# The MLP's down projection as seven products of halves, woven between the up projection's tiles

## The chip, the core and the metric

The kernel runs on one core of a Trainium2 chip. The metric is the device time of one execution in microseconds (us). The core has five engines that run side by side and wait for each other through semaphores: TensorE (PE in the profile, its weight loads PEld) multiplies matrices and writes to the eight banks of PSUM; VectorE (DVE), ScalarE (ACT) and GpSimd (POOL) work element by element; SyncE (SP) issues most transfers (DMAs) from HBM into SBUF. Each engine executes its own queue strictly in order.

## The reference

One encoder layer is applied to two groups of 256 tokens with shared weights: three attention branches with gates, an output projection, and then the part that matters here, an MLP with a squared ReLU between two RMS norms. All is float32.

```
    x = x + merged @ w_out
    h2 = rms_norm(x, norm2_g)
    x = x + jnp.square(jax.nn.relu(h2 @ w_up)) @ w_down
    ...
    return rms_norm(x, final_norm_g)
```

D_MODEL is 1024, D_FF is 4096; both groups together are 512 tokens. `w_up` is 1024 x 4096 and `w_down` 4096 x 1024.

## The kernel before

**Precision.** Every large product is made of three matmuls on operands that are split into a high and a low half (`mm3`, line 182): high times high, high times low, low times high. The high half is the operand rounded by a ScalarE copy to TensorE's fast type; the low half is the rest, formed by a subtraction on VectorE. Activations are split in the same way when they are made.

**The order of work.** The program is a list of units. `unit(fn, *srcs)` appends a function and the weight chunks that it needs, and `run` (line 168) executes the list: it sees to it that a unit's chunks are fetched, calls it, and then fetches the chunks of the next units, `ahead` of them (three during the MLP, four at its end). To fetch a chunk (`chunk`, line 160) is to load 128 x 1024 values into one of two `raw` buffers by SyncE, to copy them to `hi` on ScalarE and to subtract into `lo` on VectorE (`halves`). `hi` and `lo` come from ten `w` buffers.

VectorE, ScalarE and TensorE are wrapped in `InOrder` (line 62): what they execute is in the order in which the program writes it. GpSimd (`G`) and SyncE (`SP`) are not wrapped; a planner decides when their instructions come in their queues, and it also hands out the buffers of a pool and puts in every wait. A tile that is taken from a full pool waits for the last reader of the tile whose place it gets.

**The MLP** starts at line 817. The residual `X1` (1024 x 512, features on partitions) and the split activations `H` stand ready.

- `up` (line 837) makes one tile of 128 rows of the hidden layer for all 512 tokens: 24 matmuls (`fm`, 8 x 3), then the ReLU out of the bank on ScalarE, the square on VectorE, and its two halves (`u`).
- `turn_x1` (line 821) transposes the residual on TensorE, after the first eight up tiles, into the sums `acc`, which have tokens on partitions; ScalarE also forms the sums of squares for the norm (`ss`; `inv_ms` makes `rr` from them). The norm's factor is applied at the end: `rr` scales the down projection's result.
- The hidden layer is worked off in four quarters of 1024 (`qq`). After a quarter's eight up tiles come its down products (`tm`, line 194): for each half of the 1024 outputs, four chunks of weights, each with 24 matmuls (four token tiles x two blocks of 128 x three), into four banks. Then `add_down` adds a bank, times `rr`, to `acc` by one VectorE instruction per token tile.
- The last half of the last quarter is `last_down` (line 877): it takes its four chunks first and goes token tile by token tile, with the last tile in two halves of 256 columns. After each token tile `final` normalizes it and sends it out: reduction and scaling on VectorE, the power on GpSimd, then ScalarE and VectorE scale a half each, and two DMAs write it.

`flush` executes what was put into the list `later`: work out of banks that is issued behind the next unit's matmuls.

Of the kernel before, what the change touches and what calls it, by code (L numbers as in the profile page):

```python
# [77 lines left out]
def encoder_kernel(ctx: ExitStack, tc: tile.TileContext, a: dict, out: bass.AP):  # L78
    nc = tc.nc
    V, A, E = (InOrder(tc, e) for e in (nc.vector, nc.scalar, nc.tensor))  # L80
    G, SP = nc.gpsimd, nc.sync

    sb = ctx.enter_context(tc.tile_pool(name="sb", bufs=1))
    ps = ctx.enter_context(tc.tile_pool(name="ps", bufs=8, space=bass.MemoryType.PSUM))
    dr = ctx.enter_context(tc.tile_pool(name="dr", bufs=1, space=bass.MemoryType.DRAM))

    cnt = [0]

    def nm(s):
        cnt[0] += 1  # L90
        return f"{s}{cnt[0]}"

    def s4(s="s"):
        return sb.tile([P, 2, T], F32R, tag="s4", name=nm(s), bufs=21)

    def h2(s="h", dt=F32):
        return sb.tile([P, T], dt, tag="h2", name=nm(s), bufs=20)

    def bank(s="ps"):
        return ps.tile([P, 512], F32, tag="ps", name=nm(s))  # L100

    def const(s, shape, dt=F32):
        return sb.tile(shape, dt, name=s, tag=s, bufs=1)
# [4 lines left out]
    def f(x):  # L108
        return x.bitcast(F32)

    def wide(s):
        return sb.tile([P, 512], F32, tag="bias", name=nm(s), bufs=3, padded_shape=[P, 768])

    PHS = ((0, 4), (4, NPH))
    oh = [wide("oh") for _ in PHS]
# [21 lines left out]
    p = bank("warm")  # L137
# [6 lines left out]
    def unit(fn, *srcs):  # L144
        units.append((fn, srcs))

    def raw_tile():
        return sb.tile([P, 1024], F32, tag="raw", name=nm("raw"), bufs=2)

    def w_tile():  # L150
        return sb.tile([P, 1024], F32R, tag="w", name=nm("w"), bufs=10)
# [8 lines left out]
    def chunk(src, n=1024):  # L160
        raw, hi, lo = raw_tile(), w_tile(), w_tile()
        SP.dma_start(raw[:, :n], src)
        halves(raw, hi, lo, slice(0, n))
        return hi, lo

    ahead = [1]

    def run():
        need = [(i, s) for i, (_, srcs) in enumerate(units) for s in srcs]
        got, at = [[] for _ in units], 0  # L170
        done = 0
        for i, (fn, srcs) in enumerate(units):
            done += len(srcs)
            for fetch in (True, False):
                while at < min(len(need), done + (0 if fetch else ahead[0])):
                    u, s = need[at]
                    got[u].append(chunk(*s))
                    at += 1
                if fetch:
                    fn(*got[i])  # L180

    def mm3(o, wh, wl, xh, xl, first, last):
        E.matmul(o, wh, xh, start=first, stop=False)
        E.matmul(o, wh, xl, start=False, stop=False)
        E.matmul(o, wl, xh, start=False, stop=last)

    def fm(w, X, o):

# [70 lines left out]
    later = []  # L259
# [170 lines left out]


    def sm_tile():
        return sb.tile([P, 2, 384], F32, tag="sp", name=nm("sp"), bufs=3)

    def bias_tile():
        return sb.tile([P, 2, 384], F32, tag="bias", name=nm("bias"), bufs=3)

    biases = []

# [99 lines left out]
            E.matmul(o, QQ[:, e, c], K[:, e, k], start=(n == 0), stop=(n == 1))  # L539

    def turn_two(s):
        t = sb.tile([P, 2, 512], F32R, tag="pT", name=nm("pT"), bufs=2)
        two(turn(s, 0, 2), t[:, 0], t[:, 1])
        return t

# [109 lines left out]
    def flush(n=2):  # L655
        for fn in later[:n]:
            fn()
        del later[:n]
# [45 lines left out]
    def put_v12(t, p):  # L704

        b, i = divmod(t, 2)
        for rl in range(2):
            v = sb.tile([P, S], F32, tag="v12", name=nm("v12"), bufs=8)
            A.activation(v[HALF[0]], p[HALF[rl], :S], AF.Copy)
            V.tensor_copy(v[HALF[1]], p[HALF[rl], S:])  # L710
            V12[b, 2 * i + rl] = v
# [102 lines left out]
        unit(out_proj, (a["w_o"][ff],))  # L814


    acc = {}
    ss = const("ss", [P, NT, 2])
    rr = const("rr", [P, NT])

    def turn_x1(t, hh):

        b = bank("tp")
        for i in range(4):
            E.transpose(b[:, i * P:(i + 1) * P], X1[4 * hh + i][:, t * P:(t + 1) * P], ident)
        acc[t, hh] = h2("acc")
        A.activation(acc[t, hh], b, AF.Copy)
        A.activation(wide("junk"), b, AF.Square, accum_out=ss[:, t, hh:hh + 1])

    def inv_ms():  # L830
        V.tensor_tensor(rr, ss[:, :, 0], ss[:, :, 1], op=ALU.add)
        V.tensor_scalar(rr, rr, 1.0 / D, EPS, op0=ALU.mult, op1=ALU.add)
        V.reciprocal(rr, rr)

    U = {}

    def up(w, qq, ff):
        p = bank()
        fm(w, H, p)
        r = h2("r")  # L840
        A.activation(r, p, AF.Relu)
        V.tensor_tensor(r, r, r, op=ALU.mult)
        u = s4("u")
        A.activation(u[:, 0], r, AF.Copy)
        V.tensor_tensor(u[:, 1], r, f(u[:, 0]), op=ALU.subtract)
        U.setdefault(qq, []).append(u)

    gf = []
    fs = const("fs", [P, NT, 3])
    fr = const("fr", [P, NT])  # L850

    def load_gf():
        for hh in range(2):
            g = wide("gf")
            A.dma_start(g, bass.AP(tensor=a["gf"].tensor, offset=a["gf"].offset + hh * T, ap=[[0, P], [1, T]]))
            gf.append(g)

    def add_down(t, hh, p, last=False):
        y = acc[t, hh]
        V.scalar_tensor_tensor(y, p, rr[:, t:t + 1], y, op0=ALU.mult, op1=ALU.add)  # L860
        if last:
            A.activation(wide("junk"), y, AF.Square, accum_out=fs[:, t, 0:1])
            V.tensor_tensor(y, y, gf[hh], op=ALU.mult)

    def final(t, c, n):
# [4 lines left out]
        G.tensor_tensor(r, r, mhalf[:, 0:1], op=ALU.pow)  # L870
        V.tensor_tensor(acc[t, 1][:, c], acc[t, 1][:, c], gf[1][:, c], op=ALU.mult)
        A.activation(acc[t, 0], acc[t, 0], AF.Copy, scale=r)
        V.tensor_scalar(acc[t, 1], acc[t, 1], r, None, op0=ALU.mult)
        for hh in range(2):
            (A, SP)[hh].dma_start(out[t * P:(t + 1) * P, hh * 512:(hh + 1) * 512], acc[t, hh])

    def last_down(*ws):

        flush(NT)
        Uq = U[3]  # L880
        for t in range(NT):
            c = slice(t * P, (t + 1) * P)
            cols = ((0, 512),) if t < NT - 1 else ((0, 256), (256, 512))
            for part, (n0, n1) in enumerate(cols):
                p = bank()[:, :n1 - n0]
                for k in range(KD):
                    wh, wl = ws[k // 2]
                    w = slice((k % 2) * 512 + n0, (k % 2) * 512 + n1)
                    mm3(p, Uq[k][:, 0, c], Uq[k][:, 1, c], wh[:, w], wl[:, w], k == 0, k == KD - 1)
                y = acc[t, 1][:, n0:n1]  # L890
                V.scalar_tensor_tensor(y, p, rr[:, t:t + 1], y, op0=ALU.mult, op1=ALU.add)
                A.activation(wide("junk")[:, n0:n1], y, AF.Square, accum_out=fs[:, t, 1 + part:2 + part])
                if n1 < 512:
                    V.tensor_tensor(y, y, gf[1][:, n0:n1], op=ALU.mult)
            final(t, slice(n0, n1), 1 + len(cols))

    for qq in range(4):
        for ff in range(KD):
            unit(lambda w, qq=qq, ff=ff: up(w, qq, ff), (a["w_up"][8 * qq + ff],))
            if qq == 0:  # L900
                unit(lambda ff=ff: turn_x1(ff // 2, ff % 2))
        if qq == 0:
            unit(inv_ms)
            unit(load_gf)
        uq = U.setdefault(qq, [])
        if qq == 3:
            unit(lambda: ahead.__setitem__(0, 4))
        for hh in range(2):
            srcs = [a["w_dn"][qq, hh, i] for i in range(4)]
            if qq == 3 and hh:  # L910
                unit(last_down, *[(s,) for s in srcs])
            else:
                def after(t, p, hh=hh, qq=qq):
                    if qq < 3:
                        add_down(t, hh, p)
                    else:
                        later.append(lambda: add_down(t, hh, p, True))

                for u in tm(uq, srcs, 512, after):
                    unit(*u)  # L920
    run()


# [72 lines left out]
```

## Time and profile before

| what | us |
|---|---|
| median of three runs | 872.12 (872.07 to 872.5) |
| the profiled execution's own time | 871.41 |
| its span, first to last instruction | 869.6 |
| first up tile's first matmul | 510.88 |
| last matmul of the MLP ends | 863.30 |

The span is the time from the first to the last instruction; the execution's own time has 1.8 us more around it. In the profile a line of a group names the source line, the engine, the operation, what is written from what (`w<-raw,w` is the low half of a weight, `ps` a bank), the shapes, the count, and then busy time, mean duration in ns, and the idle time of the engine just before with what ended it. Source line 72 is the wrapper of `InOrder`, so operations on the three wrapped engines are told apart by their tiles. Matmuls are pipelined: the recorded duration of one is longer than the pace at which they follow each other, which is read from the chain of work or from the timeline.

### The profile page before, as it was taken

What the parts mean: (1) busy time and instruction counts of PE and PEld (TensorE: products, weight loads), DVE (VectorE), ACT (ScalarE), POOL (GpSimd) and SP (SyncE); (2) the same over time, 40 slices, a digit from 0 to 9 for tenths busy, and PEclk for the clock granted to TensorE, in tenths of its full rate; (3) what the DMA queues carried; (4) which work ended last, traced back from release to release, by engine and by line L of the source; (5) the groups of instructions that cost most, each with busy time, mean ns of one, the idle gap of its engine ahead of it and who ended that gap; (6) DMA issues with size and microseconds to landing.
All of it is one profiled execution on the core that took longest, in us unless ns stands there. A gap on an engine that the chain in (4) does not pass through costs nothing.

```text
span 869.6 us, 10683 instructions
## 1 busy us (share of the span) xinstructions
PE 858.7 (99%) x4176; PEld 717.3 (82%) x4176; DVE 390.1 (45%) x625; ACT 344.7 (40%) x606; POOL 192.6 (22%) x133
## 2 busy tenths in 40 slices
PE   9999999999999999999999999999999999999997
PEld 8778998888888888888887888888888888888886
DVE  6595445456443213333436444433453345334543
ACT  6364555565654332232224335521342144214432
POOL 2315455547556551112212000000000000000001
PEclk9999999999999999999999999999999999999999
DMA  8342223233332122222323432332223222322222
GB/s 284 113 136 88 83 73 103 80 93 98 106 94 71 51 87 96 96 86 97 121 73 99 149 117 96 122 119 74 95 98 121 74 95 98 123 73 93 97 77 98
DMA packets 41851, 88.00 MB, mean 101 GB/s; under 512 B 18734, under 2 KB 18980, under 8 KB 41800
## 3 DMA queue, kind: packets, MB, share of 16 engines
q1 hardware_dynamic: 39272, 83.07, 29.3%
q10 hardware_dynamic: 2304, 4.20, 1.5%
q8 instruction: 33, 0.54, 0.3%
q14 instruction: 18, 0.15, 0.1%
q0 software_dynamic: 224, 0.05, 0.0%
HBM read 85.15 MB, written 2.14 MB: 100 GB/s over the span
## 4 chain that ended last, share of the span: by engine, by line
PE 88%; DVE 4%; ACT 2%; DMA 2%; issue 2%; POOL 1%; SPq 0%; POOLq 0%; DVEq 0%; ACTq 0%
PE ps L72 81%; PE sc L72 3%; PE o L72 2%; PE tp L72 2%; DMA mr<-in_memT 1%; DMA raw<-in_w_mem 1%; ACT sp L72 1%; DVE sp L72 1%; DVE w L72 1%; DVE mg L72 0%; ACT w L72 0%; DVE st L72 0%; DVE qq L72 0%; DVE kl L72 0%; DVE sq L72 0%
## 5 line engine op out<-in xcount | busy, mean ns | idle before, releaser
L72 PE MATMUL ps<-x,w 128*128 128x512 f32 x1080 | 252.4, 391 | 0.0
L72 PEld LDWEIGHTS ps<-x,w 128*128 128x128 f32 x1080 | 200.8, 188 | 41.5
L72 DVE TENSOR_TENSOR w<-raw,w 128x1024 fp32r<-128x1024 f32 (+1 forms) x107 | 131.3, 1234 | 128.7 <-ACT w L72 128.6
L72 ACT ACTIVATE w<-raw 128x1024 fp32r<-128x1024 f32 (+2 forms) x144 | 149.1, 1040 | 95.4 <-DMA raw<-in_w_dn 37.4
L72 PE MATMUL ps<-h,w 128*128 128x512 f32 x768 | 176.7, 390 | 0.0
L72 PE MATMUL ps<-w,u 128*128 128x512 f32 (+1 forms) x792 | 175.1, 383 | 0.0
L72 PEld LDWEIGHTS ps<-w,u 128*128 128x128 f32 x792 | 145.5, 188 | 29.0
L72 PEld LDWEIGHTS ps<-h,w 128*128 128x128 f32 x768 | 143.6, 188 | 29.6
L158 POOL TENSOR_TENSOR w<-raw,w 128x1024 fp32r<-128x1024 f32 (+1 forms) x37 | 87.3, 2361 | 117.8 <-ACT w L72 95.0
L870 POOL TENSOR_TENSOR fr<-fr,mhalf 128x1 f32<-128x1 f32 x4 | 3.5, 870 | 395.9 <-DVE fr L72 395.9
L72 ACT ACTIVATE r<-ps 128x512 f32<-128x512 f32 x32 | 19.1, 598 | 114.4 <-PE ps L72 114.4
L72 DVE TENSOR_TENSOR r<-r 128x512 f32<-128x512 f32 x32 | 22.1, 692 | 70.8 <-ACT r L72 70.8
L72 ACT ACTIVATE sp<-sp,st 128x256 f32<-128x256 f32 (+1 forms) x48 | 25.8, 538 | 57.7 <-DVE st L72 57.7
L72 DVE SCALAR_TENSOR_TENSOR acc<-ps,rr,acc 128x512 f32<-128x512 f32 (+1 forms) x33 | 24.2, 733 | 54.3 <-PE ps L72 54.3
L72 PE MATMUL ps<-mg,w 128*128 128x512 f32 x192 | 44.3, 390 | 1.5 <-ACT mg L72 0.9
L72 ACT ACTIVATE g<-ps 128x512 f32<-128x512 f32 x16 | 9.6, 598 | 91.0 <-PE ps L72 91.0
L72 PEld LDWEIGHTS ps<-mg,w 128*128 128x128 f32 x192 | 36.0, 188 | 9.6 <-ACT mg L72 1.3
L72 PE MATMUL ps<-w,x 128*128 128x384 f32 (+1 forms) x192 | 39.9, 363 | 0.0
L72 DVE TENSOR_TENSOR sum<-o,lo 64x256 f32<-64x256 f32 x24 | 10.0, 418 | 66.5 <-ACT lo L72 66.4
L457 POOL TENSOR_TENSOR sp<-sp,st 128x512 f32<-128x512 f32 (+1 forms) x32 | 36.7, 1147 | 6.5 <-DVE st L72 3.6
L72 PEld LDWEIGHTS ps<-w,x 128*128 128x128 f32 x192 | 34.3, 188 | 3.6
L72 DVE TENSOR_TENSOR u<-r,u 128x512 fp32r<-128x512 f32 x32 | 22.2, 692 | 22.4 <-ACT u L72 22.4
(135 smaller groups left out, 814.4 us busy)
## 6 DMA issues: line engine op xcount, KB each, us to landing
raw<-in_w_up SPq DMA_DIRECT2D x32, 512.0 KB, 3.2
raw<-in_w_dn SPq DMA_DIRECT2D x32, 512.0 KB, 3.3
raw<-in_w_g SPq DMA_DIRECT2D x24, 512.0 KB, 3.3
raw<-in_w_b SPq DMA_DIRECT2D x12, 512.0 KB, 3.2
raw<-in_w_bam SPq DMA_DIRECT2D x8, 512.0 KB, 3.2
raw<-in_w_o SPq DMA_DIRECT2D x8, 512.0 KB, 3.3
raw<-in_w_mem SPq DMA_DIRECT2D x7, 512.0 KB, 4.3
bias<-scr SPq DMA_DIRECT2D x48, 64.0 KB, 3.0
```

The costliest lines, as they stand in the source:

```text
L72: return self.tc.keep_in_program_order(method(*args, **kw))
L158: sub[0].tensor_tensor(lo[:, c], raw[:, c], f(hi[:, c]), op=ALU.subtract)
L457: G.tensor_tensor(s[:, :, :w], s[:, :, :w], st[:, 6:8].unsqueeze(2).to_broadcast([P, 2, w]), op=ALU.mult)
L870: G.tensor_tensor(r, r, mhalf[:, 0:1], op=ALU.pow)
```

## The change

Seven products of halves take the place of eight (Strassen's scheme in a form with shared sums). The hidden layer is now worked off in eight chunks `c` of 512. For each, the 512 tokens, the 512 hidden rows and the 1024 outputs are each cut in two halves, and the product of a 2 x 2 by a 2 x 2 arrangement of blocks is made from seven products of blocks and sums of blocks. A product is 2 (token tiles) x 2 (blocks of 128) x 3 matmuls of 512 columns, twelve in all.

- `up` keeps the square in float32, and makes it on GpSimd. The split into halves is moved to `form`.
- `load_blocks(c)`, called in the third up tile of each chunk, loads the chunk's four weight blocks (128 x 1024 each, the same bytes as before) into eight `blk` buffers and makes four sums of them on GpSimd: a, b, c, d. `parts` splits one of the seven into halves when it is fetched, three units ahead, as other weights are.
- `form(c, n)` makes the left operand of product n: for n = 0 four sums on GpSimd, and for each n the split of one form on ScalarE and VectorE.
- The order of units in loop step c: the four up tiles of chunk c, then the seven products of chunk c - 1, after each of them `form(c, n)`. The last step has the seven products of chunk 7 alone.
- `product` puts P1, Q5, Q6 and P7 into new pairs of banks (a, d, c, e); P2 goes on in P1's pair, Q3 in Q5's and Q4 in P7's. After its matmuls it flushes what the product before left: two sums on VectorE, each adding a bank to one of five accumulators of two tiles (`add_to`; the first use of an accumulator is a copy on ScalarE, which may carry the sign).
- In the last step `last_sums` takes the place of `add_to`: it puts the accumulators together, scales them by `rr` onto the residual and, for the last four products, ends the four token tiles (`finish`, `final`).
- The transposed residual is written to DRAM by `turn_x1` (now after the up tiles of chunks 0 and 1) and fetched again before the last products (`fetch_x1`). Buffers that only attention used are given back, and the `blk` buffers take their place (`mlp_pool`).

The core of the diff:

```
+    def load_blocks(c):
+        t = {n: block_tile() for n in ("11", "12", "a", "22", "b", "c", "21", "d")}
+        for n, (k, h) in (("11", (0, 0)), ("12", (0, 1)), ("22", (1, 1)), ("21", (1, 0))):
+            SP.dma_start(t[n], a["w_dn"][c // 2, h, 2 * (c % 2) + k])
+        G.tensor_tensor(t["a"], t["11"], t["12"], op=ALU.add)
+        G.tensor_tensor(t["b"], t["a"], t["22"], op=ALU.add)
+        G.tensor_tensor(t["c"], t["12"], t["22"], op=ALU.add)
+        G.tensor_tensor(t["d"], t["b"], t["21"], op=ALU.add)
+        blocks[c] = t
...
     def up(...):
...
-        V.tensor_tensor(r, r, r, op=ALU.mult)
-        u = s4("u")
-        A.activation(u[:, 0], r, AF.Copy)
-        V.tensor_tensor(u[:, 1], r, f(u[:, 0]), op=ALU.subtract)
+        G.tensor_tensor(UP[c, m // 2][:, m % 2], r, r, op=ALU.mult)
+        if m == 2:
+            load_blocks(c)
...
+    def parts(c, n):
+        def go():
+            hi, lo = w_tile(), w_tile()
+            src = blocks[c][n]
+            A.activation(hi, src, AF.Copy)
+            V.tensor_tensor(lo, src, f(hi), op=ALU.subtract)
+            return hi, lo
+        return go
...
+    def form(c, n):
+        lo, hi = UP[c, 0], UP[c, 1]
+        A11, A21, A12, A22 = lo[:, :, :S], lo[:, :, S:], hi[:, :, :S], hi[:, :, S:]
+        if n == 0:
+            for m in (1, 2, 4, 5):
+                forms[c, m] = h2("f").rearrange("p (j t) -> p j t", j=2)
+            G.tensor_tensor(forms[c, 1], A21, A22, op=ALU.subtract)
+            G.tensor_tensor(forms[c, 2], A11, forms[c, 1], op=ALU.subtract)
+            G.tensor_tensor(forms[c, 4], A11, A21, op=ALU.subtract)
+            G.tensor_tensor(forms[c, 5], A12, forms[c, 2], op=ALU.subtract)
+        src = {0: A11, 3: A12, 6: A22}[n] if n in (0, 3, 6) else forms[c, n]
+        x = s4("f")
+        xh, xl = (x[:, i].rearrange("p (j t) -> p j t", j=2) for i in range(2))
+        A.activation(xh, src, AF.Copy)
+        V.tensor_tensor(xl, src, f(xh), op=ALU.subtract)
+        forms[c, n] = x
+
+    def add_to(k, i, p, op=ALU.add):
+        if (k, i) in acc:
+            V.tensor_tensor(acc[k, i], acc[k, i], p, op=op)
+        else:
+            acc[k, i] = h2("acc")
+            A.activation(acc[k, i], p, AF.Copy, scale=1.0 if op == ALU.add else -1.0)
+
+    PRODUCTS = (("P1", "11", "a", ("V", -1)), ("Q5", "a", "d", ("G", 1)), ("Q6", "b", "c", ("V", 1)),
+                ("P2", "21", "a", ("11", 1)), ("P7", "c", "e", ("G", -1)), ("Q3", "22", "d", ("12", 1)),
+                ("Q4", "d", "e", ("21", 1)))
+
+    def product(w, c, n):
+        name, _, bk, (to, sign) = PRODUCTS[n]
+        x = forms.pop((c, n))
+        new = name in ("P1", "Q5", "Q6", "P7")
+        for i in range(2):
+            if new:
+                banks[bk, i] = bank()
+            p = banks[bk, i]
+            for j in range(2):
+                t = slice(j * S + i * P, j * S + (i + 1) * P)
+                k = slice(j * 512, (j + 1) * 512)
+                mm3(p, x[:, 0, t], x[:, 1, t], w[0][:, k], w[1][:, k], new and j == 0, j == 1, not new)
+        flush(9)
+        ps_ = [banks[bk, i] for i in range(2)]
+        if c < NC - 1:
+            later.append(lambda: [add_to(to, i, ps_[i], ALU.add if sign > 0 else ALU.subtract) for i in range(2)])
+        else:
+            later.append(lambda: last_sums(name, ps_))
...
+    def last_sums(name, ps_):
+        for i in range(2):
+            p, lo, hi = ps_[i], i, i + 2
+            y = {(t, hh): xt[t][:, hh] for t in (lo, hi) for hh in range(2)}
+            if name == "P1":
+                scaled(y[lo, 0], lo, 0, acc["11", i])
+                add_to("V", i, p, ALU.subtract)
+            elif name == "Q5":
+                add_to("G", i, p)
+            elif name == "Q6":
+                add_to("V", i, p)
+                for k in ("12", "G"):
+                    V.tensor_tensor(acc[k, i], acc[k, i], acc["V", i], op=ALU.add)
+                V.tensor_tensor(acc["21", i], acc["21", i], acc["V", i], op=ALU.subtract)
+                scaled(y[lo, 1], lo, 1, acc["12", i])
+                scaled(y[hi, 1], hi, 1, acc["G", i])
+                scaled(y[hi, 0], hi, 0, acc["21", i])
+            elif name == "P2":
+                finish(lo, 0, y[lo, 0], p)
+            elif name == "P7":
+                finish(hi, 1, y[hi, 1], p, -1)
+            elif name == "Q3":
+                finish(lo, 1, y[lo, 1], p)
+                final(lo)
+            else:
+                finish(hi, 0, y[hi, 0], p)
+                final(hi)
+
+    def finish(t, hh, y, p, sign=1):
+        scaled(y, t, hh, p, sign)
+        A.activation(h2("junk"), y, AF.Square, accum_out=fs[:, t, hh:hh + 1])
+        V.tensor_tensor(y, y, gf[0][:, hh], op=ALU.mult)
...
+    for c in range(NC + 1):
+        if c < NC:
+            for m in range(4):
+                unit(lambda w, ff=4 * c + m: up(w, ff), (a["w_up"][4 * c + m],))
...
+        for n in range(7):
+            unit(lambda w, c=c - 1, n=n: product(w, c, n), (parts(c - 1, PRODUCTS[n][1]),))
+            if c < NC:
+                unit(lambda c=c, n=n: form(c, n))
+    unit(lambda: flush(9))
```

`scaled` is one VectorE instruction: source times `rr` (or minus `rr`), plus the residual tile. `final` adds the two sums of squares, scales (VectorE), takes the power (GpSimd), scales a half each on ScalarE and VectorE, and sends both out.

More of the change, by code (lines that the diff above doesn't have):

```diff
@@ L85, in encoder_kernel @@
     dr = ctx.enter_context(tc.tile_pool(name="dr", bufs=1, space=bass.MemoryType.DRAM))
+    stages = ExitStack()
+    at = [stages.enter_context(tc.tile_pool(name="at", bufs=1))]
+    ctx.callback(stages.close)
     cnt = [0]
@@ L111, in wide @@
     def wide(s):
-        return sb.tile([P, 512], F32, tag="bias", name=nm(s), bufs=3, padded_shape=[P, 768])
+        return at[0].tile([P, 512], F32, tag="bias", name=nm(s), bufs=3, padded_shape=[P, 768])
     PHS = ((0, 4), (4, NPH))
@@ L176, in run @@
                     u, s = need[at]
-                    got[u].append(chunk(*s))
+                    got[u].append(s[0]() if callable(s[0]) else chunk(*s))
                     at += 1
@@ L180, in run, with mm3 @@
                     fn(*got[i])
[L182 to L185, printed above, removed]
+    def mm3(o, wh, wl, xh, xl, first, last, more=False):
+        E.matmul(o, wh, xh, start=first, stop=False, skip_group_check=more)
+        E.matmul(o, wh, xl, start=False, stop=False, skip_group_check=more)
+        E.matmul(o, wl, xh, start=False, stop=last, skip_group_check=more)
     def fm(w, X, o):
@@ L432, in sm_tile @@
     def sm_tile():
-        return sb.tile([P, 2, 384], F32, tag="sp", name=nm("sp"), bufs=3)
+        return at[0].tile([P, 2, 384], F32, tag="sp", name=nm("sp"), bufs=3)
     def bias_tile():
-        return sb.tile([P, 2, 384], F32, tag="bias", name=nm("bias"), bufs=3)
+        return at[0].tile([P, 2, 384], F32, tag="bias", name=nm("bias"), bufs=3)
     biases = []
@@ L541, in turn_two @@
     def turn_two(s):
-        t = sb.tile([P, 2, 512], F32R, tag="pT", name=nm("pT"), bufs=2)
+        t = at[0].tile([P, 2, 512], F32R, tag="pT", name=nm("pT"), bufs=2)
         two(turn(s, 0, 2), t[:, 0], t[:, 1])
@@ L707, in put_v12 @@
         for rl in range(2):
-            v = sb.tile([P, S], F32, tag="v12", name=nm("v12"), bufs=8)
+            v = at[0].tile([P, S], F32, tag="v12", name=nm("v12"), bufs=8)
             A.activation(v[HALF[0]], p[HALF[rl], :S], AF.Copy)
@@ L814, in encoder_kernel, with mlp_pool, block_tile @@
         unit(out_proj, (a["w_o"][ff],))
-    acc = {}
+    NC = 8
     ss = const("ss", [P, NT, 2])
     rr = const("rr", [P, NT])
+    nr = const("nr", [P, NT])
+    fs = const("fs", [P, NT, 2])
+    fr = const("fr", [P, NT])
+    x1d = dr.tile([NT, P, D], F32, name="x1d")
+    def mlp_pool():
+        stages.close()
+        at[0] = stages.enter_context(tc.tile_pool(name="ml", bufs=1))
+    def block_tile():
+        return at[0].tile([P, 1024], F32, tag="blk", name=nm("blk"), bufs=8)
     def turn_x1(t, hh):
@@ L825, in turn_x1 @@
             E.transpose(b[:, i * P:(i + 1) * P], X1[4 * hh + i][:, t * P:(t + 1) * P], ident)
-        acc[t, hh] = h2("acc")
-        A.activation(acc[t, hh], b, AF.Copy)
-        A.activation(wide("junk"), b, AF.Square, accum_out=ss[:, t, hh:hh + 1])
+        x = h2("xt")
+        A.activation(x, b, AF.Copy)
+        A.activation(h2("junk"), b, AF.Square, accum_out=ss[:, t, hh:hh + 1])
+        A.dma_start(x1d[t, :, hh * 512:(hh + 1) * 512], x)
     def inv_ms():
@@ L833, in inv_ms, with up @@
         V.reciprocal(rr, rr)
-    U = {}
-    def up(w, qq, ff):
+        V.tensor_scalar(nr, rr, -1.0, None, op0=ALU.mult)
+    UP, blocks = {}, {}
+    def up(w, ff):
+        c, m = divmod(ff, 4)
+        if m % 2 == 0:
+            UP[c, m // 2] = sb.tile([P, 2, T], F32, tag="s4", name=nm("u"), bufs=21)
         p = bank()
@@ L841, in up @@
         A.activation(r, p, AF.Relu)
-        V.tensor_tensor(r, r, r, op=ALU.mult)
-        u = s4("u")
-        A.activation(u[:, 0], r, AF.Copy)
-        V.tensor_tensor(u[:, 1], r, f(u[:, 0]), op=ALU.subtract)
[L846 to L865, printed above, removed]
+        G.tensor_tensor(UP[c, m // 2][:, m % 2], r, r, op=ALU.mult)
[10 more added lines that the diff above has]
+        blocks[c] = t
@@ new lines, in parts @@
+    def parts(c, n):
[6 more added lines that the diff above has]
+        return go
+    forms = {}
+    def form(c, n):
[14 more added lines that the diff above has]
+        forms[c, n] = x
@@ new lines, in encoder_kernel @@
+    acc, banks = {}, {}
+    def add_to(k, i, p, op=ALU.add):
[7 more added lines that the diff above has]
+                ("Q4", "d", "e", ("21", 1)))
@@ new lines, in encoder_kernel, with fetch_x1, scaled @@
+    xt, gf = {}, []
+    def fetch_x1():
+        for t in range(NT):
+            xt[t] = sb.tile([P, 2, 512], F32, tag="s4", name=nm("xt"), bufs=21)
+            SP.dma_start(xt[t], x1d[t].rearrange("p (h n) -> p h n", h=2))
+        g = sb.tile([P, 2, 512], F32, tag="s4", name=nm("gf"), bufs=21)
+        SP.dma_start(g, bass.AP(tensor=a["gf"].tensor, offset=a["gf"].offset, ap=[[0, P], [T, 2], [1, T]]))
+        gf.append(g)
+    def scaled(y, t, hh, src, sign=1):
+        V.scalar_tensor_tensor(y, src, (rr if sign > 0 else nr)[:, t:t + 1], y, op0=ALU.mult, op1=ALU.add)
@@ L867, in final @@
+    def finish(t, hh, y, p, sign=1):
+        scaled(y, t, hh, p, sign)
+        A.activation(h2("junk"), y, AF.Square, accum_out=fs[:, t, hh:hh + 1])
+        V.tensor_tensor(y, y, gf[0][:, hh], op=ALU.mult)
+    def final(t):
         r = fr[:, t:t + 1]
-        V.tensor_reduce(r, fs[:, t, :n], axis=AX.X, op=ALU.add)
+        V.tensor_tensor(r, fs[:, t, 0:1], fs[:, t, 1:2], op=ALU.add)
         V.tensor_scalar(r, r, 1.0 / D, EPS, op0=ALU.mult, op1=ALU.add)
         G.tensor_tensor(r, r, mhalf[:, 0:1], op=ALU.pow)
-        V.tensor_tensor(acc[t, 1][:, c], acc[t, 1][:, c], gf[1][:, c], op=ALU.mult)
@@ L872, in final @@
-        A.activation(acc[t, 0], acc[t, 0], AF.Copy, scale=r)
-        V.tensor_scalar(acc[t, 1], acc[t, 1], r, None, op0=ALU.mult)
+        A.activation(xt[t][:, 0], xt[t][:, 0], AF.Copy, scale=r)
+        V.tensor_scalar(xt[t][:, 1], xt[t][:, 1], r, None, op0=ALU.mult)
         for hh in range(2):
[L875 to L920, printed above, removed]
+            (A, SP)[hh].dma_start(out[t * P:(t + 1) * P, hh * 512:(hh + 1) * 512], xt[t][:, hh])
@@ new lines, in encoder_kernel @@
+    unit(mlp_pool)
+    for c in range(NC + 1):
+        if c < NC:
+            for m in range(4):
+                unit(lambda w, ff=4 * c + m: up(w, ff), (a["w_up"][4 * c + m],))
+                if c == 0:
+                    unit(lambda m=m: turn_x1(m, 0))
+                if c == 1:
+                    unit(lambda m=m: form(0, m))
+                    unit(lambda m=m: turn_x1(m, 1))
+                if c == 2 and m == 0:
+                    unit(inv_ms)
+        if c == 1:
+            for n in range(4, 7):
+                unit(lambda n=n: form(0, n))
+        if c == 0:
+            unit(lambda: ahead.__setitem__(0, 3))
+            continue
+        if c == NC:
+            unit(fetch_x1)
+        for n in range(7):
+            unit(lambda w, c=c - 1, n=n: product(w, c, n), (parts(c - 1, PRODUCTS[n][1]),))
+            if c < NC:
+                unit(lambda c=c, n=n: form(c, n))
```

## The prediction

> **What bounds the kernel now.** I read the page's totals, then the chain that ended last in order of time, then the groups by shape, then the timeline of the end.
>
> ```profile
> span 869.6 us, 10683 instructions
> ...
> PE 858.7 (99%) x4176; PEld 717.3 (82%) x4176; DVE 390.1 (45%) x625; ACT 344.7 (40%) x606; POOL 192.6 (22%) x133
> 516.92 5.47 PE ps L72 x24
> 522.39 0.44 PE tp L72 x4
> 558.33 299.24 PE ps L72 x1320
> 857.57 0.02 issue
> 510.88 5.61 PE L72 MATMUL ps<-h,w 128*128 128x512 f32 x24
> 862.78 0.52 PE L72 MATMUL ps<-w,u 128*128 128x256 f32 x3
> L72 PE MATMUL ps<-h,w 128*128 128x512 f32 x768 | 176.7, 390 | 0.0
> L72 PE MATMUL ps<-w,u 128*128 128x512 f32 x744 | 169.4, 389 | 0.0
> L72 PE MATMUL ps<-w,u 128*128 128x256 f32 x48 | 5.9, 283 | 0.0
> ```
>
> The MLP runs from 510.88 us (first up tile) to 863.30 (last matmul, 862.78 + 0.52). In it TensorE never stops: one piece of the chain holds 1320 matmuls in 299.24 us, so a 512-wide matmul costs 0.2267 us of path (its recorded 390 ns is pipelined). The last token tile's 48 half-wide ones took 863.30 - 857.57 = 5.73. All else hides, until the last 6.3 us to the end of the span at 869.6.
>
> **What is removed.** The down projection has 744 + 48 matmuls; seven products of 2 x 2 x 3 in each of eight chunks make 672 wide ones. Gone are 72 x 0.2267 = 16.3 and 5.7: **-22.0 us**. The up tiles and the eight transposes stay. That gain is real only if the others keep pace with a product, 12 x 0.2267 = 2.72 us, where a pair of weight halves served 24 matmuls before.
>
> **What is added to VectorE.**
>
> ```profile
> L72 DVE TENSOR_TENSOR w<-raw,w 128x1024 fp32r<-128x1024 f32 x64 | 77.8, 1224 | 44.7 <-ACT w L72 44.7
> L72 DVE TENSOR_TENSOR u<-r,u 128x512 fp32r<-128x512 f32 x32 | 22.2, 692 | 22.4 <-ACT u L72 22.4
> 467.21 1.28 DVE L72 TENSOR_TENSOR g<-ps,g 128x512 f32<-128x512 f32 x2
> L72 ACT ACTIVATE w<-raw 128x1024 fp32r<-128x1024 f32 x64 | 66.9, 1050 | 77.1 <-DMA raw<-in_w_dn 37.4 <-DMA raw<-in_w_up 20.4 <-PE ps L72 19.3
> L72 ACT ACTIVATE u<-r 128x512 fp32r<-128x512 f32 x32 | 20.2, 633 | 24.3 <-DVE r L72 24.3
> L72 ACT ACTIVATE r<-ps 128x512 f32<-128x512 f32 x32 | 19.1, 598 | 114.4 <-PE ps L72 114.4
> ```
>
> Between two products it executes, in written order: **D**, two sums from banks (like g<-ps,g, two in 1.28); **S**, the low half of a weight (1.22), three units ahead; **F**, the low half of the next chunk's form (0.69). Sum 3.19 against 2.72: over seven products 22.3 against 19.0. An up tile needs only one S in 24 x 0.2267 = 5.44, so the lag heals there. ScalarE needs 1.05 + 0.63 per product, less than 2.72. POOL gets four squares, four form sums (1.29 each, from a row below) and four block sums (2.42): 20 us of a chunk's 180 x 0.2267 = 41. Those two are no bound by themselves.
>
> The lag bites at one wait. P7 and Q4 share a bank pair (e), with only Q3 between. Q4 may not write until VectorE has summed P7, and that D is queued behind everything of the products before it. Let 0 be the start of P1; Q4 is due at 6 x 2.72 = 16.3. S of the third product can start at 1.7 (relu 0.60, copy 1.05, behind the last up tile). Up to the first half of P7's D stand 6 S, 5 F, 5 D and 0.69: 1.7 + 7.3 + 3.5 + 6.4 + 0.7 = 19.6. So even undisturbed Q4 waits 3.3 us. What is queued behind Q4 on TensorE is the next up tile.
>
> **POOL gets in the way.**
>
> ```profile
> L72 DVE TENSOR_TENSOR mg<-g,mg x5: 679/1777/1786, 461.5 to 471.5; 128x512 fp32r<-128x512 f32 x5
> L783 POOL TENSOR_TENSOR mg<-g,mg x3: 1295/1749/1750, 461.4 to 464.4; 128x512 fp32r<-128x512 f32 x3
> 461.49 5.80 DVE L72 TENSOR_TENSOR mg<-g,mg 128x512 fp32r<-128x512 f32 x4
> L72 DVE TENSOR_TENSOR g<-ps,g x16: 675/692/692, 337.7 to 467.8; 128x512 f32<-128x512 f32 x16
> L158 POOL TENSOR_TENSOR w<-raw,w 128x1024 fp32r<-128x1024 f32 x33 | 80.0, 2424 | 104.4 <-ACT w L72 84.8 <-DVE mk L72 19.4
> L773 POOL TENSOR_TENSOR g<-g,g 128x512 f32<-128x512 f32 x7 | 9.1, 1293 | 92.0 <-DVE g L72 92.0
> raw<-in_w_dn SPq DMA_DIRECT2D x32, 512.0 KB, 3.3
> ```
>
> At 461.5, where merge splits on both engines at once, VectorE's 0.68 becomes 1.78 and POOL's 1.30 becomes 1.75: each waits out the other's instruction, in turn. Both read two SBUF tiles. S and F are of that kind, and so are POOL's squares and form sums (1.29 each) and block sums (2.42). D has one input in a bank; that form never exceeded 0.69. The Trainium skill, "SBUF — State Buffer", Who interferes with whom, states this as an exclusive lock for a whole instruction, for a VectorE operation with two SBUF inputs and not for one; by it the sum is the 940 below, without it the 896 of a rival.
>
> POOL's four form sums are ready at 2.0, after the square of the last up tile. Its sums b, c, d for the next chunk need block 22, whose buffer is free only after this chunk's S for Q3, plus 3.3 to land: S ends at 14.7, so b could start at 18.0, and finds F ahead of it until 18.6. Walked with alternation (end of each VectorE step, POOL in brackets):
> S 3.2 [form sum 4.5], D(Q4 before) 4.5, S 5.7 [7.0], F 7.7, D(P1) 9.0 [9.0], S 10.2 [11.5], F 12.2, D(Q5) 13.5, S 14.7, F 15.4, D(Q6) 16.7, S 17.9, F 18.6 [b 21.0], D(P2) 19.9, S 22.2 [c 24.6], F 25.3, D(P7) 26.0 and 26.6.
> Q4 runs 26.0 to 28.7 instead of ending at 19.0: **+9.7** in each of six full phases, 58.2. In the first phase ten sums go to ScalarE as first copies, four D fewer (5.1) before P7's: Q4 starts near 20.9, **+4.6**. Bounds per full phase: 3.3 (no contention) and, if POOL's two rounds and the clock (below) come on top, about 12.
>
> **The end.** The last two rows of products stand back to back, with no up tiles to heal the lag.
>
> ```profile
> 857.59 0.75 DVE L72 SCALAR_TENSOR_TENSOR acc<-ps,rr,acc 128x512 f32<-128x512 f32 x1 [2.01 <-PE ps L72]
> 859.13 0.15 DVE L72 TENSOR_REDUCE fr<-fs 128x1 f32<-128x2 f32 x1 [0.79 <-ACT junk L72]
> 859.32 0.15 DVE L72 TENSOR_SCALAR fr<-fr 128x1 f32<-128x1 f32 x1
> 859.56 0.93 POOL L870 TENSOR_TENSOR fr<-fr,mhalf 128x1 f32<-128x1 f32 x1 [4.49 <-DVE fr L72]
> 860.52 0.49 DVE L72 TENSOR_SCALAR acc<-acc,fr 128x512 f32<-128x512 f32 x1 [0.44 <-POOL fr L870]
> 865.52 0.48 DVE L72 TENSOR_SCALAR acc<-acc,fr 128x512 f32<-128x512 f32 x1 [0.44 <-POOL fr L870]
> ```
>
> From scaling a tile (857.59) VectorE waits for ScalarE's square until 859.13 (1.54); the gain multiply, in line there, adds 0.69: 2.23 per tile for P2 and P7. For Q3 and Q4 each half also makes a token tile final: 859.13 to 861.01, 1.88 more, 4.1 together. VectorE's list: Q4's old D 1.28, P1 2 x (0.75 + 0.69) = 2.9, Q5 1.28, Q6 2 x (4 x 0.69 + 3 x 0.75) = 10.0, four S 4.9, P2 and P7 8.9, Q3 and Q4 16.4: 45.7. After the last scaling 869.6 - 866.0 = 3.6 remain (output). VectorE enters 32.8 - 28.7 = 4.1 late (after P7's D: d until 27.7, S 28.9, F 29.6, D 30.9, S 32.1, F 32.8). End at 53.4 from the start of these products; TensorE alone would end at 19.0 + 6.3 = 25.3: **+28.1**. Back-to-back instructions start up to 0.08 early, worth 2 to 3 of this; the end has no other cover.
>
> **Clock.**
>
> ```profile
> 863.40:866.00 2.60, 0.00 (x0) 0.00 (x0) 1.55 (x5) 0.99 (x3) 0.66 (x1) 0.90 0.00 0
> 866.00:869.60 3.60, 0.00 (x0) 0.00 (x0) 0.01 (x1) 0.24 (x1) 0.00 (x0) 0.50 0.38 146
> ```
>
> With TensorE idle from 863.30 the granted clock is halved from about 865.5. A wait of 9.7 would reach that; no row shows matmuls behind such an idle time. Bounds for seven waits: 0 and 7 x 2.72 = 19 (each Q4 at half speed). I take 0, since in every row with matmuls the clock was 1.00, and keep 19 for the range. The Trainium skill, "TensorE: Matmul & The Clock Gate", Part 1, gives about 3.4 us at half rate after such a pause; an estimate by that page is 1.7 per wait, 12 in all, and the sum would be 952.
>
> **Costed at nothing:** the x1 round trip through DRAM and its DMAs (beside up tiles; late fetches have 19 us of products), the same 32 down loads, bank slots (each product's new pair finds four free), the pool change. Without cover the fetch would cost some 3 us once.
>
> **Sum**, against the profiled execution's own 871.4 (span 869.6 and 1.8 around it; the median of the runs is 872.1, 0.7 above): 871.4 - 22.0 + 58.2 + 4.6 + 28.1 = **940**.
>
> **Rivals.**
> - *The block sums fall elsewhere.* If b, c, d run under the up tiles, the walk loses their two waits: D(P7) reaches half at 22.5, Q4 ends at 25.2, 6 x 6.2 + 1.1 = 38; entry to the end 3.0 late, 27. 871.4 - 22 + 38 + 27 = 914. For it: POOL's order is the planner's. Against: block 22 comes free in the middle of the products.
> - *No contention worth counting*: 6 x 3.3 = 20, and 27: 896. Against: the mg rows.
> - *Faster: VectorE's order isn't the written one.* If P7's D is done by 16.3 (that is the deciding point) nothing waits, and if the waits for squares (8 x 0.85) and powers (4 x 0.96) at the end are filled, 45.7 becomes 35, +13 with no lag: 871.4 - 22 + 13 = 862. For it: TensorE has 99% and VectorE 45%. Against: VectorE is issued in written order, and 3.19 per product is over 2.72 in either order.
> - *Worse*: clock and ScalarE's queue waiting for POOL's forms: 952 to 975.
>
> **Chances.** Forecast 0.46, block sums elsewhere 0.22, no contention 0.12, worse 0.12, faster 0.07, within 0.2% 0.01. About 0.2% is what a measurement of this kernel can tell from no change. Slower 0.92. The range 888 to 965 takes in 896, 914, 940 and the clock's 19; it leaves out faster, and the worst.
>
> **What would show it.** Right: TensorE idle once per chunk before Q4, released by VectorE's sum of P7; S and F stretched to 2 us or more beside POOL; after the last matmul VectorE busy for 15 us or more. Wrong: TensorE still at 99%, or the idle time before another product, or released by a weight split or a DMA.

## The result, and the profile after

| | before | after |
|---|---|---|
| median (range), us | 872.25 (872.07 to 872.5, 4 runs) | 963.44 (961.51 to 964.04, 4 runs) |
| ratio | | 1.1041, 95% interval 1.1022 to 1.1061 |
| profiled execution (span), us | 871.41 (869.6) | 961.51 (959.6) |
| TensorE instructions | 4176 | 4056 |

The change makes the kernel 10.4% slower, although it takes away 120 matmuls, as it says (744 + 48 - 672). The page of the changed kernel, its totals and its slices (tenths busy of 40 equal slices; PEclk is the granted clock):

```profile
span 959.6 us, 10832 instructions
...
PE 862.4 (90%) x4056; PEld 712.0 (74%) x4056; DVE 518.6 (54%) x724; ACT 381.3 (40%) x662; POOL 384.2 (40%) x229
...
PE   9999999999999999999999997959597795959582
...
PEclk9999999999999999999999998979899897979795
```

TensorE has holes at even distances from the 25th slice on (576 us); the first product begins at 558.68. In the changed kernel the seven products of a chunk stand in a row, behind four up tiles. The view of the waits sums up what TensorE's matmuls waited for (us in total, times, longest):

```profile
PE ps L72 <- DVE acc L72: 64.3, 7, 9.7
PE ps L72 <- DVE xt L72: 6.6, 1, 6.6
PE ps L72 <- DVE w L72: 5.4, 8, 2.0
```

Seven waits for VectorE's sums out of banks, one in each row of products but the last, which waits for `xt`. The timeline of TensorE and then of VectorE over one chunk in the middle:

```profile
694.17 5.46 PE L72 MATMUL ps<-w,f 128*128 128x512 f32 x12 [9.67 <-DVE acc L72]
699.42 22.38 PE L72 MATMUL ps<-h,w 128*128 128x512 f32 x96
721.64 13.99 PE L72 MATMUL ps<-w,f 128*128 128x512 f32 x61
736.13 2.81 PE L72 MATMUL ps<-w,f 128*128 128x512 f32 x11 [0.50 <-DVE w L72]
748.59 4.35 PE L72 MATMUL ps<-w,f 128*128 128x512 f32 x12 [9.65 <-DVE acc L72]
```

```profile
724.56 1.28 DVE L72 TENSOR_TENSOR acc<-acc,ps 128x512 f32<-128x512 f32 x2
...
728.60 1.27 DVE L72 TENSOR_TENSOR acc<-acc,ps 128x512 f32<-128x512 f32 x2
...
732.65 1.27 DVE L72 TENSOR_TENSOR acc<-acc,ps 128x512 f32<-128x512 f32 x2
733.84 2.23 DVE L72 TENSOR_TENSOR w<-blk,w 128x1024 fp32r<-128x1024 f32 x1
736.00 2.88 DVE L72 TENSOR_TENSOR f<-f,f 128x512 fp32r<-128x512 f32 x1
738.80 1.27 DVE L72 TENSOR_TENSOR acc<-acc,ps 128x512 f32<-128x512 f32 x2
740.00 2.17 DVE L72 TENSOR_TENSOR w<-blk,w 128x1024 fp32r<-128x1024 f32 x1
742.09 2.82 DVE L72 TENSOR_TENSOR f<-u,f 128x512 fp32r<-128x512 f32 x1
744.84 1.27 DVE L72 TENSOR_TENSOR acc<-acc,ps 128x512 f32<-128x512 f32 x2
...
747.77 1.27 DVE L72 TENSOR_TENSOR acc<-acc,ps 128x512 f32<-128x512 f32 x2
```

Read them together. The four up tiles (x96) end at 721.6, where P1 begins. Six products follow; the last twelve matmuls of a chunk, Q4's, start 9.65 us late, at 748.59. VectorE runs through without a pause meanwhile; its sums come in the order Q4 of the chunk before, P1, Q5, Q6, P2, P7. The first of P7's two sums ends at about 748.45 (747.77 and 0.68), and Q4 starts 0.14 behind it. A form's low half that needs 0.68 alone takes 2.88 at 736.00. POOL's timeline shows what stands against it there:

```profile
723.63 2.17 POOL L902 TENSOR_TENSOR f<-u,u 128x512 f32<-128x512 f32 x1
725.88 2.25 POOL L903 TENSOR_TENSOR f<-u,f 128x512 f32<-128x512 f32 x1
728.09 1.76 POOL L904 TENSOR_TENSOR f<-u 128x512 f32<-128x512 f32 x1
729.80 2.37 POOL L905 TENSOR_TENSOR f<-u,f 128x512 f32<-128x512 f32 x1
732.14 2.86 POOL L878 TENSOR_TENSOR blk<-blk,blk 128x1024 f32<-128x1024 f32 x1
735.08 3.26 POOL L879 TENSOR_TENSOR blk<-blk,blk 128x1024 f32<-128x1024 f32 x1
738.30 2.79 POOL L880 TENSOR_TENSOR blk<-blk,blk 128x1024 f32<-128x1024 f32 x1
741.16 3.20 POOL L881 TENSOR_TENSOR blk<-blk,blk 128x1024 f32<-128x1024 f32 x1
```

All eight sums of the next chunk lie in one piece inside the products, and each is stretched too. Beside them six of VectorE's low halves are stretched (1.79, 1.79, 2.23, 2.88, 2.17, 2.82), by 8.5 us in all over the 0.68 and 1.22 that they take alone. Without these 8.5 us Q4 would start 18.4 us after P1, where it is due at 16.3; this is worked out from the rows and tried below. The last step's end, TensorE and VectorE:

```profile
909.32 22.12 PE L72 MATMUL ps<-w,f 128*128 128x512 f32 x84 [9.66 <-DVE acc L72]
938.02 5.13 PE L72 MATMUL ps<-w,f 128*128 128x512 f32 x12 [6.58 <-DVE xt L72]
...
955.26 0.49 DVE L72 TENSOR_SCALAR xt<-xt,fr 128x512 f32<-128x512 f32 x1 [0.66 <-POOL fr L997]
```

The last matmul ends at 943.2; VectorE works until 955.75, 12.6 us longer.

**Where the time went**, from span to span:

| step | worked out from | us |
|---|---|---|
| matmuls gone | 72 x 0.2267 + 5.7 | -22.0 |
| first row of products | P1 at 558.68, Q4 at 586.35: 27.7 instead of 16.3 | +11.4 |
| six full chunks | Q4 at 586.35 to Q4 at 909.32: 322.97, less 6 x 180 x 0.2267 = 244.84 | +78.1 |
| the end | 959.6 - 909.32 - 2.72 = 47.6, less 25.3 | +22.3 |
| sum | | +89.8 |

The spans differ by 959.6 - 869.6 = 90.0.

### The profile page after: what moved, and what is told of

Its sections match the earlier page's. It is cut to its first block, busy times and chain, and to the rows that moved or that the text cites. A ratio compares the mean times of both kernels' runs of the same rounds, so it can differ in the third digit from the quotient of the medians.

```text
span 959.6 us, 10832 instructions
## 1 busy us (share of the span) xinstructions
PE 862.4 (90%) x4056; PEld 712.0 (74%) x4056; DVE 518.6 (54%) x724; ACT 381.3 (40%) x662; POOL 384.2 (40%) x229
## 4 chain that ended last, share of the span: by engine, by line
PE 69%; DVE 19%; issue 5%; ACT 4%; DMA 2%; POOL 0%; SPq 0%; POOLq 0%; DVEq 0%; ACTq 0%
PE ps L72 63%; DVE f L72 7%; DVE w L72 4%; DVE acc L72 3%; PE sc L72 2%; PE o L72 2%; PE tp L72 2%; DVE xt L72 1%; DMA mr<-in_memT 1%; ACT w L72 1%; DMA raw<-in_w_mem 1%; ACT sp L72 1%; DVE sp L72 1%; DVE sq L72 0%; ACT junk L72 0%
## 5 line engine op out<-in xcount | busy, mean ns | idle before, releaser
L72 PE MATMUL ps<-w,f 128*128 128x512 f32 x672 | 177.9, 427 | 76.3 <-DVE acc L72 64.3
L72 PEld LDWEIGHTS ps<-w,f 128*128 128x128 f32 x672 | 138.7, 209 | 113.2 <-issue 74.0
L72 DVE TENSOR_TENSOR w<-raw,w 128x1024 fp32r<-128x1024 f32 (+1 forms) x75 | 93.1, 1244 | 151.1 <-ACT w L72 151.0
L72 ACT ACTIVATE w<-raw 128x1024 fp32r<-128x1024 f32 (+2 forms) x112 | 115.9, 1038 | 113.1 <-DMA raw<-in_w_up 90.3
L869 POOL TENSOR_TENSOR u<-r 128x512 f32<-128x512 f32 x32 | 33.3, 1042 | 249.7 <-ACT r L72 249.7
L72 DVE TENSOR_TENSOR w<-blk,w 128x1024 fp32r<-128x1024 f32 x56 | 85.9, 1535 | 87.0 <-ACT w L72 87.0
L72 ACT ACTIVATE w<-blk 128x1024 fp32r<-128x1024 f32 x56 | 58.5, 1054 | 21.7 <-DVE f L72 12.8
L72 DVE TENSOR_TENSOR acc<-acc,ps 128x512 f32<-128x512 f32 x94 | 60.1, 677 | 0.0
L72 DVE TENSOR_TENSOR f<-f,f 128x512 fp32r<-128x512 f32 x32 | 43.7, 1368 | 0.0
L72 DVE TENSOR_TENSOR f<-u,f 128x512 fp32r<-128x512 f32 x24 | 41.3, 1720 | 0.0
```

The lines of the kernel that those rows point to most:

```text
L72: return self.tc.keep_in_program_order(method(*args, **kw))
L869: G.tensor_tensor(UP[c, m // 2][:, m % 2], r, r, op=ALU.mult)
```

## The experiments

The theory: a row of seven products lets VectorE fall behind; Q4 is the matmul that feels it first, since it shares P7's banks; POOL's sums make up a good part of the lag by holding back VectorE's two-input instructions; the halved clock after each wait is on the path; and the end is VectorE's list. The rivals: the shared bank alone is at fault, VectorE's own work is the whole lag, the clock costs nothing, or contention makes VectorE late wherever the products stand. Where a run is single, its one time stands against 961.5 to 964.0 for the changed kernel.

### A bank pair for Q4 (one run)

```
-        new = name in ("P1", "Q5", "Q6", "P7")
+        new = name in ("P1", "Q5", "Q6", "P7") or (name == "Q4" and c < NC - 1)
...
+            if name == "P7":
+                later.append(lambda: [add_to("21", i, ps_[i]) for i in range(2)])
```

> Q4 gets a bank pair of its own in chunks 0 to 6, and P7's and Q4's banks are both added to the accumulator 21 (two more sums on VectorE per chunk, 1.3 us); the last chunk is left as it is. If the shared bank is what makes TensorE wait, the seven waits before Q4 (64.3 us together) and their half-clock matmuls (some 2.5 us each) go, while VectorE's lag stays and heals under the up tiles: 875 to 895 us. Rival: the lag itself is the bound, and another wait (weights, a free bank, the end) takes its place: above 925 us.

Measured: 926.04 us, a miss: 31 us above what was expected, and just inside the rival's time. The long waits are gone (nine for sums, 1.5 at most), but the view of TensorE's waits now has others:

```profile
PE ps L72 <- DVE w L72: 24.7, 23, 2.1
PE ps L72 <- DVE xt L72: 11.4, 1, 11.4
PE ps L72 <- DVE acc L72: 7.0, 9, 1.5
```

The shared bank is the place where the lag is felt first, and it makes the lag dearer: 35 to 38 us go with it, with shorter waits and a mean clock of 0.971 instead of 0.947. It is not the cause of the rest: TensorE now waits 23 times for weight splits that stand in the same queue of VectorE.

### Matmuls that nobody needs, to keep the clock (one run)

```
+        if name == "Q4":
+            q = bank("warm")
+            for i in range(40):
+                E.matmul(q, x[:, 0, :P], w[0][:, :512], start=True, stop=True)
```

> The same kernel with 40 more matmuls (512 wide, into a spare bank that nobody reads) ahead of each Q4: 40 x 0.2267 = 9.1 us of work inside an idle time of 9.7. If the half clock after the idle time is on the path, each Q4 runs at full rate again and six phases win 2.5 us each, less about 3 in the first, whose wait is only 6.3: 945 to 950 us, with eight times forty more matmuls. Rival: VectorE sets the pace of the next phase too, and the clock costs nothing: 960 us or more.

Measured: 951.04 us, 10 to 13 us faster with 320 more matmuls; 1 us outside what was expected, on the slow side. The windows of the changed kernel (Q4 after its wait, then the up tiles) and of this one (a whole chunk); the number before the last two is the granted clock:

```profile
640.00:645.20 5.20, 5.20 (x12) 4.10 (x13) 5.12 (x7) 1.58 (x2) 0.00 (x0) 0.50 0.52 195
645.20:667.20 22.00, 22.00 (x97) 18.17 (x96) 3.68 (x3) 4.64 (x6) 3.13 (x3) 0.99 0.27 91
```

```profile
640.00:694.00 54.00, 52.79 (x232) 43.06 (x231) 36.42 (x36) 16.92 (x22) 24.75 (x12) 1.00 0.26 88
```

Q4's twelve matmuls take 5.2 us at clock 0.50, not 2.72. Kept busy, TensorE stays at 1.00. So the halved clock is on the path, and worth 10 to 13 us of the 90.

### POOL's sums left out (one run each)

The blocks (`t.update({"a": t["11"], "b": t["12"], "c": t["22"], "d": t["21"]})`), and in the second run the forms too (`forms.update({(c, 1): A21, (c, 2): A11, (c, 4): A21, (c, 5): A12})`), are used as they are, without the sums; what these two kernels multiply is no longer the layer, and only their times and traces are of use.

> GpSimd's four block sums a, b, c, d are left out; the blocks 11, 12, 22, 21 stand in their places. If the instructions of GpSimd stretch VectorE's in the products, the wait before Q4 falls from 9.7 to about 6 us: 930 to 942 us. Rival: VectorE's own work is the whole lag: 958 us or more.

> GpSimd's four block sums and four form sums per chunk are left out, with blocks and parts of the squares in their places; GpSimd keeps the squares. VectorE's work is unchanged. With contention as the main part of the lag, the wait before Q4 falls to about 3 us and the clock may stay whole: 890 to 920 us. Rival: VectorE's own work is the whole lag: 955 us or more.

Measured: 914.55 and 890.85 us. The first is a miss by 15 us to the fast side: its seven waits are 25.9 us together, where seven of the expected 6 would be 42. The second is where it was expected, at the fast end. TensorE's waits for sums out of banks, first without block sums, then without either:

```profile
PE ps L72 <- DVE acc L72: 25.9, 7, 4.1
```

```profile
PE ps L72 <- DVE acc L72: 12.2, 7, 1.9
```

VectorE's work is the same in all three. TensorE's longest wait falls from 9.7 to 4.1 to 1.9, so four fifths of it are POOL's doing; what VectorE lacks by its own work is the last 1.9, near the 2.1 that the rows above leave (18.4 less 16.3). In the last run VectorE's low half of a form is back at 0.69 and of a weight at 1.22. The runs leave out POOL's results as well as its instructions, but VectorE is not kept waiting for those results in the changed kernel (no pause from 723.42 to 748.45); it is the stretch that goes.

### P7 one product earlier (one run)

```
-        for n in range(7):
+        for n in (0, 1, 2, 4, 3, 5, 6):
```

> P7 changes places with P2, so that two products stand between P7 and Q4 and its sums are written one product earlier for VectorE. All work is the same. If the queue in front of P7's sums is the cause, the wait before Q4 falls from 9.7 to about 3 us and the clock is mostly kept: 890 to 915 us. Rival: the lag moves to the next wait (weights of Q3 or Q4, a free bank): above 940 us.

Measured: 946.84 us, a miss, in the time of the rival but not by its reason: the wait stays before Q4 and falls only to 6.7.

```profile
677.80 2.88 DVE L72 TENSOR_TENSOR f<-f,f 128x512 fp32r<-128x512 f32 x1
...
683.89 2.82 DVE L72 TENSOR_TENSOR f<-f,f 128x512 fp32r<-128x512 f32 x1
686.64 1.27 DVE L72 TENSOR_TENSOR acc<-acc,ps 128x512 f32<-128x512 f32 x2
687.83 1.21 DVE L72 TENSOR_TENSOR w<-raw,w 128x1024 fp32r<-128x1024 f32 x1
```

P7's sums (686.64) are now one place earlier in VectorE's queue, but behind all of the steps that POOL's block sums stretch. Only a place whose steps take their bare 3 us was passed. The expectation of about 3 fits the prediction's walk, in which this place took 6.1 us (19.9 to 26.0) because the block sums came later there.

### A plain end (one run)

The last chunk is multiplied out with eight products, token tile by token tile; the accumulators are put together first.

```
+    def plain(*ws):
+        flush(9)
+        gather()
+        for t in range(NT):
...
+                for j in range(4):
+                    mm3(p, US[j][:, 0, c], US[j][:, 1, c], wh[:, w], wl[:, w], j == 0, j == 3)
+                finish(t, hh, xt[t][:, hh], p)
+            final(t)
```

> Only the end is changed: the last chunk of 512 is multiplied out without the seven products (96 matmuls, 12 more, 2.7 us), token tile by token tile, with the accumulators put together while TensorE works. If VectorE's list of last sums is what the end costs (about 22 us over TensorE's own), and the last row of products, which has no forms beside it, waits less: 928 to 940 us. Rival: the end is bound by something that stays (transfers of the residual, the last token tile): above 950 us.

Measured: 943.2 us, 18 to 21 faster; 3 us outside the expectation, on the slow side: VectorE still enters the end late and spends 5.7 us per token tile where TensorE needs 5.4.

### The products woven between the up tiles (one run), and both together

The products stand two, two, two, one behind the four up tiles, instead of seven in a row. All work is the same; with the order of the products, each form's split is moved to two products ahead of its use, and the sums are flushed behind up tiles too. The run doesn't tell these three apart.

```
+    SLOTS = ((0, 1), (2, 3), (4, 5), (6,))
...
+            unit(lambda w, ff=4 * c + m: up(w, ff), (a["w_up"][4 * c + m],))
+            unit(lambda: flush(9))
...
+                for n in SLOTS[m]:
+                    prod(c - 1, n)
```

> Only the order of units is changed: two products between one up tile and the next (two, two, two, one), each form made two products ahead of its use, and the sums flushed behind up tiles too. All work is the same, but VectorE's 3.2 us per product now meets 2.72 + 2.72 of TensorE. If the lag inside a row of seven products is the cause, the waits before Q4 and the half clock go (64 + 17 us): 868 to 885 us, the end as before. Rival: contention alone makes VectorE late wherever the products stand: above 910 us.

> The woven order and the plain end together: 84 x 0.2267 = 19 us of matmuls saved against the kernel before. If the two causes found are all there is: 850 to 858 us, faster than both kernels. Rival: a new wait in the middle or at the end: 865 us or more.

Measured: 877.63 us for the order alone, as expected: 84 to 86 us are back with the same work on every engine (TensorE 4056 matmuls, VectorE 724 instructions, POOL 229). Two chunks of it by windows (TensorE, weight loads, VectorE, ScalarE, POOL), and VectorE's weight splits there:

```profile
617.60:658.40 40.80, 40.80 (x181) 33.78 (x181) 31.51 (x33) 16.57 (x23) 23.54 (x13) 1.00 0.31 104
658.40:699.20 40.80, 40.80 (x181) 33.78 (x181) 31.52 (x33) 16.56 (x23) 23.54 (x13) 1.00 0.32 103
```

```profile
L72 DVE TENSOR_TENSOR w<-blk,w 128x1024 fp32r<-128x1024 f32 x29 | 43.7, 1506 | 12.3 <-ACT w L72 12.3
```

TensorE has no gap, and a chunk takes 40.80 us, which is 180 x 0.2267. The contention is still there (1506 ns per split, 1.22 us alone), but now it hides; it is also less, since VectorE is busy for 495.8 us in all instead of 518.6. The waits that are left, 12.4 us, stand in the last row of products, from 818.9 on. With the plain end: 872.27 us, ratio 1.0003 (0.9993 to 1.0013), no difference to the kernel before, and not the 850 to 858 expected: a miss. The trace has the rest at the end: a wait of 6.5 us for a ScalarE split that stood behind a late weight load, and 16.1 us from the last matmul (852.9) to the end of the span (869.0) instead of 6.3.

### The end mended (4 runs)

The residual is fetched a chunk earlier, the last hidden tile is split ahead of Q4, the accumulators are put together in three steps, two of them between the last up tiles, and a token tile's gain multiplies stand behind both of its scalings.

```
+            if c == NC - 1 and m >= 2:
+                unit(lambda m=m: gather(m - 2))
...
+                scaled(xt[t][:, hh], t, hh, p)
+                square_sum(t, hh)
+            V.tensor_tensor(y[:, 0], y[:, 0], gf[0][:, 0], op=ALU.mult)
```

> The woven order and the plain end again, with the two faults that the trace of woven_plain_end shows taken away: the residual is fetched a chunk earlier into buffers of the weight blocks, the last hidden tile is split ahead of Q4 (the 6.5 us wait for ScalarE before the last products), and the accumulators are put together in three steps between the last up tiles, with the gain multiplies of a token tile behind both of its scalings (VectorE ran 5.7 us per token tile against TensorE's 5.4 and entered 9 us late; the span ended 16.1 us after the last matmul instead of 6.3). TensorE: 1452 matmuls x 0.2267 + 3.5 from 510.5 ends at 843; with 7 us behind it and 2 around the span: 850 to 856 us. Rival: the woven order has no more to give and the end stays late: 864 us or more.

Measured: 859.82 us (858.6 to 861.89) against 872.44, ratio 0.986 (0.9836 to 0.9883): 1.4% faster than the kernel before, some 4 us short of what was expected. TensorE's last rows:

```profile
820.29 2.98 PE L72 MATMUL ps<-w,f 128*128 128x512 f32 x12 [1.18 <-DVE acc L72]
823.11 1.98 PE L72 MATMUL ps<-w,u 128*128 128x512 f32 x8
827.59 21.86 PE L72 MATMUL ps<-w,u 128*128 128x512 f32 x88 [2.50 <-DVE u L72]
```

Two waits, 3.7 us, are left where the last products meet the plain chunk; behind the last matmul (849.45) stand 7.4 us.

## Why the prediction was right, point by point

| step of the prediction | said | measured |
|---|---|---|
| matmuls | -22.0 | -22.0 (woven: a chunk takes 180 x 0.2267) |
| Q4's wait and what belongs to it, six full chunks | +58.2 | +78.1 |
| first row of products | +4.6 | +11.4 |
| the end | +28.1 | +22.3 |
| time of the profiled execution | 940 | 961.5 |

**The mechanism was right, the size only just.** The median of 963.44 is 23 us above the forecast and 1.6 below the end of the range. It lies in the times of the rival "worse" (952 to 975, chance 0.12), whose first half, the clock, came, and whose second, ScalarE's queue, didn't set the time: VectorE has no pause in the rows of the full chunk above. There is luck in the range: the terms of the six chunks and of the first row were too small by 20 and 7 us, that of the end too large by 6; with the end as long as forecast the time would have been 969, outside.

TensorE's long idle time in each of the six full chunks is before Q4, released by VectorE's sum of P7, as was said; the wait was put at 9.7 us, and the recorded idle time is 9.64 to 9.67. Counted as the walk counted it, from when Q4 is due, Q4 is 10.6 late (748.59 - 721.64 - 16.3). Low halves stretch beyond 2 us beside POOL (2.23, 2.88). One sign was met only in part: VectorE works 12.6 us beyond the last matmul, where 15 or more was said. The runs without POOL's sums bear out the contention, the woven order the sentence that the lag heals under up tiles.

**The clock was sized wrong.** The sum had 0 of a possible 19. From Q4's first matmul to the next up tile the six chunks take 5.02, 5.26, 5.25, 4.19, 4.97 and 5.25 us, together 29.9 instead of 16.3: 13.6 us, to which the up tiles add 0.9 more. The estimate by the Trainium skill, "TensorE: Matmul & The Clock Gate", Part 1, 1.7 per wait, was nearer (six times 1.7 is 10.2), and still low: the half rate lasts longer than the 3.4 us that it states behind five of these six waits (see the last section). The other 5.5 us of the 20 are Q4's being 10.6 late and not 9.7: 3 of them are the waits of 0.5 for weights before Q3, and the rest is put down to TensorE's filling up again after each pause, which the recorded idle time doesn't hold; this last point was not tested.

**The wait of 9.7 came out right by an order that was partly wrong, which is luck.** The walk had block sum b begin 18.6 us after P1, because block 22 was taken to need its predecessor's buffer. It begins at 735.08, 13.4 after P1, and sum a, which the walk left out, at 10.5. The old block 22 is still read then, by the split at 733.84 that ends at 736.07, so the new one had been loaded into another buffer. So the stretch lies on earlier steps: the sums of Q6 end 18.4 us after P1 (the walk had 16.7), of P2 24.5 (19.9), and the first half of P7's 26.8 (26.0). The total hardly differs, since the same sums hold back the same kind of step. What did differ is what POOL's part is worth: without the block sums the wait is 4.1, where the walk gave 6.2.

**The first row was short by 6.8** because three forms of chunk 0 were overlooked: the program has `form(0, n)` for n = 4 to 6 right behind the up tiles of chunk 1. Three more splits stand ahead of everything in VectorE's queue, beside form sums of POOL; this was read from the code and the timeline (three low halves from 562.96 to 568.1 beside POOL's form sums) and not tried by itself.

**The end was forecast too long by 5.8.** VectorE's list took 41.4 us (914.36 to 955.75), not 45.7: it starts the next instruction up to 0.08 early, and the power took 0.55 to 0.57 there instead of 0.93. It entered 2.3 us late (914.36 less 912.04, which is Q4's start and 2.72), not 4.1.

Of the other rivals, "no contention" and "block sums elsewhere" fall with the timeline of POOL; "VectorE's order isn't the written one" falls with VectorE's. The wait that "no contention" was put at, 3.3, is 1.9 in the run without POOL's sums.

## What to carry to other kernels

When an engine has room on average (VectorE 54%), ask what it has in the stretch in which its work is due: 3.2 us of it per 2.72 us of TensorE is a lag that grows product by product, another engine can multiply it (here POOL added 8.5 us to a row of seven products), and the price is paid at the first buffer that is used again. Spread the dense stretch between the sparse one before anything is optimized away; here that alone was worth 84 to 86 us with the same work. And count the end separately: the last step has no next tile to hide its sums.

## What the runs showed of the hardware that was not expected

- A pause of TensorE is paid twice. Two windows of the changed kernel, after the pause that ends at 694.17:

```profile
699.00:700.00 1.00, 1.00 (x4) 0.81 (x3) 0.29 (x1) 0.00 (x0) 0.00 (x0) 0.50 0.18 37
700.00:702.00 2.00, 2.00 (x10) 1.60 (x9) 0.00 (x0) 0.00 (x0) 0.00 (x0) 0.93 0.65 246
```

  After these 9.7 us of idling the clock stays at 0.50 for some 6 us of renewed matmuls. Behind the eight long pauses of the changed kernel (6.3 to 9.7 us) that time differs, from 2.9 us (pause ending at 748.59) to 6.1. Even a pause of 2.0 us (ending at 569.33) was followed by 3.4 us at 0.50, from 570.6 to 574.0. And 320 superfluous matmuls made the kernel 10 to 13 us faster.
- POOL's multiply of a tile by itself (line 869) takes 1.04 us (128x512), a sum of two different tiles (line 777) 1.29. Whether the single input or the operation makes the difference was not tested.
- An instruction of 0.68 us on VectorE can take 2.9 when it meets a 128x1024 sum on POOL, while VectorE's sums with one input in a bank stay at 0.68 throughout (94 of them, mean 677 ns).
